# Constant products at the start of a hybrid encoder layer, and the small products of its triangular inverses in another order

## The chip, the cores and the metric

The kernel runs on one core of a Trainium2 chip. A core has a matrix engine (TensorE, PE in the profile), three engines for element work (VectorE or DVE, ScalarE or ACT, GpSimd or POOL) and queues for transfers (SP above all). Each engine works through its own list of instructions in order and waits on semaphores. TensorE reads operands from SBUF and writes to PSUM, which has eight banks of 128 partitions by 512 f32 values. The metric is the device time of one execution in microseconds. The kernel before takes 1374.57 us, the median of three runs (1373.78 to 1376.54).

## The reference

One layer on 512 positions of width 1024, in f32, conditioned by a vector c. Cut to what matters:

```python
c_act = silu(c);  mod = c_act @ w_ada + b_ada          # nine vectors of 1024
u = rmsnorm(h, norm_ffn1) * (1 + sc1) + sh1
h = h + 0.5 * g1 * swiglu(u, w_ffn1_up, w_ffn1_down)
u = rmsnorm(h, norm_mix) * (1 + sc2) + sh2
h = h + g2 * mixer(u)       # short gated convolution + bidirectional gated DeltaNet, merged by gates
u = rmsnorm(h, norm_ffn2) * (1 + sc3) + sh3
h = h + 0.5 * g3 * swiglu(u, w_ffn2_up, w_ffn2_down)
out = rmsnorm(h, norm_final)
# DeltaNet, per head and direction, in chunks:
a_mat = strict_lower(k_beta @ k.T * decay) + I
u, w = triangular_solve(a_mat, [v * beta, k_beta * exp(g)])
# then a scan over the chunks with the state S (128 x 128)
```

## The kernel before, in words

Channels lie on the 128 partitions, the 512 positions along the free axis. A large product is done in three 128x512 passes over operands that are split in a high and a low part (lines 186 to 188 in `product_steps`); weights come as 512 KB tiles (`weight`, line 169), ScalarE makes the high part (line 174) and VectorE the low part (line 176).

The start. SP loads h; ScalarE squares its eight tiles and VectorE adds them into `ssum` (line 134). TensorE spreads c over the partitions by two products with one row (line 138), and ScalarE applies silu to get `cs`. `rstd_bcast` sums the squares over the partitions by eight products with a single column (lines 220 and 223), VectorE divides (`ms`, line 225), GpSimd raises to the power -1/2 (`rs`, line 228) and TensorE spreads the result over all partitions (line 231) into the bank kq; ScalarE copies it to `bs` (line 893). Then a loop over the eight tiles k of the width begins (lines 896 to 919). For each k VectorE multiplies two tiles of w_ada with cs (line 150), adds the bias (154), makes the scale (157), t (line 908) and the low parts ul (912) and wfl (914); ScalarE makes wfh (903) and uh (911); TensorE does 24 passes (line 918) that accumulate eight outputs in all eight banks. The first feed-forward block follows without a break.

The mixer. The order of its tasks is written out by hand in `EMIT`: letters for building a head's operands (b), inverting (i), merging (p), scanning (s) and fillers (z, g, a, m, y); large projections run between the small products. Below that a scheduler in the language's framework sets each engine's order, so an edit of one task can move instructions of others. The eight PSUM banks are: three for acc, two for ch, and one each for tp, o and kq. `build` uses tp and kq for transposes (line 481) and o and kq for the products of keys and queries (lines 547 and 548), which VectorE reads (lines 552 and 556).

The inverses. For a head there are eight 128x128 triangular matrices (four chunks of 128 positions, two directions), treated as two 64-halves of two 32-blocks each. `invert` inverts the 32x32 diagonal blocks on VectorE (lines 582 and 584). `merge` joins them: VectorE transposes blocks (line 604); the first stage multiplies, for each half b and each matrix n, a 32x32 off-diagonal block by an inverse (line 610) into the bank tp and ScalarE copies the half out (line 612); the second stage multiplies from the other side, once for the inverse (line 618) and once for its transpose (line 620), again into tp with copies (622 and 624); then 64x64 products (lines 630, 636 and 637) join the halves. A half is the partitions 0 to 63 or 64 to 127. In TensorE's terms the first stage of half 0 reads rows 32 to 63 of the array and writes columns 0 to 31, that of half 1 reads rows 96 to 127 and writes columns 64 to 95. In the second stage line 618 reads rows 0 to 31 (half 1: 64 to 95) and writes columns 0 to 31 (64 to 95), line 620 reads the same rows and writes columns 32 to 63 (96 to 127). An f32 product is two passes in the profile, each with a weight load. After the merge `scan` runs the chain over the chunks (lines 668 to 702), and line 724 transposes the result.

Of the kernel before, what the change touches and what calls it, by code (L numbers as in the profile page):

```python
# [16 lines left out]
P = 128  # L17
T = 512
# [35 lines left out]
def tile_layer(  # L54
# [24 lines left out]
    pe, act, dve, pool = nc.tensor, nc.scalar, nc.vector, nc.gpsimd  # L79
# [13 lines left out]
    psx = open_pool(ctx, "psx", bufs=1, space=PSUM)  # L93
    psum_ch = open_pool(ctx, "psum_ch", bufs=CH, space=PSUM)

    def bank(tag="acc", pool_=None):
        return (pool_ or psum).tile([P, 512], F32, tag=tag, name=tag, **({"bufs": TP} if tag == "tp" else {}))


    ones = const.tile([P, P], F32, name="ones")  # L100
    pool.memset(ones[:], 1.0)
    ident = const.tile([P, P], F32, name="ident")
# [6 lines left out]
    start = ExitStack()  # L109
# [14 lines left out]
    ssum = [sm["p"].tile([P, T], F32, tag="ssum", bufs=1, name="ssum"), None]  # L124
# [11 lines left out]
    for i in range(2):  # L136
        ps = bank("o", psx) if i else bank("ch", psum_ch)
        pe.matmul(ps[:], ones[0:1, :], crow[:, i, :], start=True, stop=True)
        act.activation(out=cs[:, T * i : T * i + T], in_=ps[:], func=ACT.Silu)


    part = const.tile([P, 72], F32, name="part")
# [69 lines left out]
    def new_sums():  # L212
        return [sm["p"].tile([P, T], F32, tag="ssum", bufs=1, name="ssum"), None]

    def rstd_bcast(sums, t0, t1, tag):

        n = (t1 - t0) // P
        ps = bank("tp", psx)
        for i in range(n):
            pe.matmul(ps[:, i : i + 1], sums[0][:, t0 + i * P : t0 + (i + 1) * P], ones[:, 0:1], start=True,  # L220
                      stop=len(sums) == 1)
            if len(sums) == 2:
                pe.matmul(ps[:, i : i + 1], sums[1][:, i * P : (i + 1) * P], ones[:, 0:1], start=False, stop=True)  # L223
        ms = sm["p"].tile([P, NC], F32, tag="ms", name="ms")
        dve.tensor_scalar(out=ms[:, 0:n], in0=ps[:, 0:n], scalar1=1.0 / D, scalar2=EPS, op0=ALU.mult,  # L225
                          op1=ALU.add)
        rs = sm["p"].tile([P, NC], F32, tag="rs", name="rs")
        pool.tensor_tensor(out=rs[:, 0:n], in0=ms[:, 0:n], in1=mhalf[:, 0:n], op=ALU.pow)  # L228
        bc = bank(tag, psx)
        for i in range(n):  # L230
            pe.matmul(bc[:, i * P : i * P + P], rs[:, i : i + 1].to_broadcast([P, P]), ident[:], start=True, stop=True)  # L231
        return bc
# [86 lines left out]
    def mixer(st, u, h, post):  # L319
# [26 lines left out]
        with ExitStack() as dd:  # L346
# [17 lines left out]
            ps = bank("ch", psum_ch)  # L364
# [16 lines left out]
            ps = bank("tp", psx)  # L381
# [31 lines left out]
            ps = bank("tp", psx)  # L413
            for d in range(2):
                pe.matmul(ps[:, 32 * d : 32 * d + 32], tri[:, d, :], g[:, d].rearrange("p c h -> p (c h)"),
                          start=True, stop=True)
# [10 lines left out]
        with dn:  # L427
# [171 lines left out]
            def merge(s, tt):  # L599
                th, tht = tt  # L600
                nl = s["nl"][:].rearrange("p d c x -> p (d c) x")
                for b in range(4):
                    co = 32 * (b % 2)
                    dve.transpose(tht[32 * b : 32 * b + 32, :, co : co + 32], th[32 * b : 32 * b + 32, :, co : co + 32])
                ps = bank("tp", psx)
                w = one.tile([P, 8, 32], F32, tag="w", bufs=2, name="w")
                for b in range(2):
                    a0, d0 = 64 * b, 64 * b + 32
                    for n in range(8):
                        pe.matmul(ps[a0 : a0 + 32, 32 * n : 32 * n + 32], nl[d0 : d0 + 32, n, a0 : a0 + 32],  # L610
                                  tht[d0 : d0 + 32, n, 32:64], start=True, stop=True)
                    act.copy(w[a0 : a0 + 32].rearrange("p a b -> p (a b)"), ps[a0 : a0 + 32, 0:256])
                yield
                ps = bank("tp", psx)
                for b in range(2):
                    a0, d0 = 64 * b, 64 * b + 32
                    for n in range(8):
                        pe.matmul(ps[a0 : a0 + 32, 32 * n : 32 * n + 32], th[a0 : a0 + 32, n, 0:32],
                                  w[a0 : a0 + 32, n, :], start=True, stop=True)
                        pe.matmul(ps[d0 : d0 + 32, 32 * n : 32 * n + 32], w[a0 : a0 + 32, n, :],  # L620
                                  th[a0 : a0 + 32, n, 0:32], start=True, stop=True)
                    act.copy(tht[a0 : a0 + 32, :, 32:64],
                             ps[a0 : a0 + 32, 0:256].rearrange("p (a b) -> p a b", a=8))
                    act.copy(th[d0 : d0 + 32, :, 0:32],
                             ps[d0 : d0 + 32, 0:256].rearrange("p (a b) -> p a b", a=8))
                yield
                w2 = one.tile([64, 8, 64], F32, tag="w2", bufs=2, name="w2")
                ps = bank("tp", psx)
                for n in range(8):
                    pe.matmul(ps[0:64, 64 * n : 64 * n + 64], nl[64:128, n, 0:64], tht[64:128, n, :],  # L630
                              start=True, stop=True)
                act.copy(w2[:].rearrange("p a b -> p (a b)"), ps[0:64, :])
                yield
                ps = bank("tp", psx)
                for c in range(NC):
                    pe.matmul(ps[0:64, 64 * c : 64 * c + 64], th[0:64, c, :], w2[:, c, :], start=True, stop=True)
                    pe.matmul(ps[64:128, 64 * c : 64 * c + 64], w2[:, NC + c, :], th[0:64, NC + c, :],
                              start=True, stop=True)
# [12 lines left out]
                pool.tensor_tensor(out=f[0:64, NC:8, 0:64], in0=th[0:64, NC:8, :], in1=sc(rki, 0), op=ALU.mult)  # L651
                pool.tensor_tensor(out=f[64:128, NC:8, 64:128], in0=th[64:128, NC:8, :], in1=sc(rki, 64),
                                   op=ALU.mult)
                dve.tensor_tensor(out=f[64:128, NC:8, 0:64], in0=pv[64:128], in1=sc(rki, 64), op=ALU.mult)
                s["f"] = f
# [232 lines left out]

    lead["p"] = open_pool(first, "lead", bufs=6, side="right")
    u = new_u()  # L890
    bc = rstd_bcast(ssum, 0, T, "kq")
    bs = sp0.tile([P, T], F32, name="bs")
    act.copy(bs[:], bc[:])
    sp1 = open_pool(start, "start_raw", bufs=RAW0)
# [148 lines left out]
```

## Time and profile before

| what | value |
|---|---|
| median of three runs | 1374.57 us |
| profiled execution, its time | 1372.99 us |
| profiled execution, its span (first to last instruction) | 1371.2 us |
| TensorE busy | 1336.6 us, 97% |
| VectorE busy | 801.8 us, 58% |
| ScalarE busy | 566.3 us, 41% |
| L610, L618, L620: passes | 256 each, 191 ns each (median) |

The profile names an instruction by line, engine, operation and tiles (written <- read). A row of the timeline has its start, its duration, and in brackets the idle time of the engine before it with what ended it. Durations of passes overlap: the pitch of a stream is the distance of starts. "x16" joins rows that follow each other. A row of the windows view has the stretch, its length, the busy time of TensorE, weight loads, VectorE, ScalarE and GpSimd with the number of instructions, the granted clock of TensorE as a fraction, the share of the transfer engines and GB/s. A row of the waits view has who waited for whom, the sum, how often, and the longest.

### The profile page before, as it was taken

What the parts mean: (1) busy time and instruction counts of PE and PEld (TensorE: products, weight loads), DVE (VectorE), ACT (ScalarE), POOL (GpSimd) and SP (SyncE); (2) the same over time, 40 slices, a digit from 0 to 9 for tenths busy, and PEclk for the clock granted to TensorE, in tenths of its full rate; (3) what the DMA queues carried; (4) which work ended last, traced back from release to release, by engine and by line L of the source; (5) the groups of instructions that cost most, each with busy time, mean ns of one, the idle gap of its engine ahead of it and who ended that gap; (6) DMA issues with size and microseconds to landing.
All of it is one profiled execution on the core that took longest, in us unless ns stands there. A gap on an engine that the chain in (4) does not pass through costs nothing. (4 is left out here: it accounts for less than half of the span.)

```text
span 1371.2 us, 19599 instructions
## 1 busy us (share of the span) xinstructions
PE 1336.6 (97%) x7417; PEld 1109.4 (81%) x7417; DVE 801.8 (58%) x1745; ACT 566.3 (41%) x1150; POOL 65.3 (5%) x103
## 2 busy tenths in 40 slices
PE   6999999999999999999999999999999999999997
PEld 4888888888888888787787777788898888888886
DVE  6865555545467989756956774657653444443333
ACT  3333333222256773665464333545433333332230
POOL 0000000000010110121111001000000000000000
PEclk9999999999999999999999999999999999999998
DMA  8646556555433543433442242557412333332331
GB/s 316 225 155 196 171 198 192 174 177 167 151 128 101 161 129 116 128 102 104 147 112 96 80 130 86 179 195 251 166 47 92 127 133 110 124 118 85 100 109 64
DMA packets 80567, 193.46 MB, mean 141 GB/s; under 512 B 24857, under 2 KB 27097, under 8 KB 80346
## 3 DMA queue, kind: packets, MB, share of 16 engines
q1 hardware_dynamic: 64984, 164.29, 38.0%
q10 hardware_dynamic: 15490, 27.94, 5.9%
q8 instruction: 58, 0.95, 0.3%
q14 instruction: 35, 0.29, 0.1%
HBM read 171.19 MB, written 21.00 MB: 140 GB/s over the span
## 5 line engine op out<-in xcount | busy, mean ns | idle before, releaser
L186 PE MATMUL acc<-uh,hi 128*128 128x512 f32 (+1 forms) x1224 | 472.5, 386 | 2.6 <-DVE sps L397 0.9
L174 ACT CAST hi<-raw 128x512 fp32r<-128x512 f32 (+1 forms) x416 | 252.1, 612 | 533.8 <-PE acc L188 486.7
L187 PE MATMUL acc<-uh,lo 128*128 128x512 f32 (+1 forms) x1224 | 471.6, 386 | 0.3 <-DVE lo L176 0.3
L188 PE MATMUL acc<-ul,hi 128*128 128x512 f32 (+1 forms) x1224 | 471.6, 386 | 0.0
L176 DVE TENSOR_TENSOR lo<-raw,hi 128x512 fp32r<-128x512 f32 (+1 forms) x416 | 279.7, 679 | 293.9 <-ACT hi L174 292.1
L186 PEld LDWEIGHTS acc<-uh,hi 128*128 128x128 f32 x1224 | 230.5, 188 | 44.1 <-ACT cacc L439 1.1
L187 PEld LDWEIGHTS acc<-uh,lo 128*128 128x128 f32 x1224 | 230.5, 188 | 41.8 <-DVE lo L176 0.5
L188 PEld LDWEIGHTS acc<-ul,hi 128*128 128x128 f32 x1224 | 230.0, 188 | 41.7
L186 PE MATMUL acc<-gh,hi 128*128 128x512 f32 (+1 forms) x396 | 144.9, 366 | 0.0
L187 PE MATMUL acc<-gh,lo 128*128 128x512 f32 (+1 forms) x396 | 144.7, 365 | 0.0
L188 PE MATMUL acc<-gl,hi 128*128 128x512 f32 (+1 forms) x396 | 144.5, 365 | 0.0
L150 DVE SCALAR_TENSOR_TENSOR raw<-raw,cs 128x1024 f32<-128x1024 f32 x72 | 88.0, 1224 | 60.2 <-DMA raw<-w_ada 60.0
L187 PEld LDWEIGHTS acc<-gh,lo 128*128 128x128 f32 x396 | 74.4, 188 | 12.2
L186 PEld LDWEIGHTS acc<-gh,hi 128*128 128x128 f32 x396 | 74.4, 188 | 12.1
L188 PEld LDWEIGHTS acc<-gl,hi 128*128 128x128 f32 x396 | 74.4, 188 | 11.8
L444 DVE SCALAR_TENSOR_TENSOR cacc<-acc,cvd_sb,cacc 128x510 f32<-128x510 f32 (+1 forms) x96 | 70.7, 741 | 1.8 <-ACT cacc L439 1.2
L313 DVE TENSOR_TENSOR sa<-sa,acc 128x512 f32<-128x512 f32 x40 | 27.4, 686 | 35.1 <-PE acc L188 33.1
L228 POOL TENSOR_TENSOR rs<-ms,mhalf 128x2 f32<-128x2 f32 (+1 forms) x7 | 6.2, 891 | 836.2 <-DVE ms L225 836.2
L196 ACT CAST gh<-sa 128x512 fp32r<-128x512 f32 x44 | 27.4, 622 | 17.9 <-DVE sa L313 13.2
L206 ACT ACTIVATE sq<-h 128x512 f32<-128x512 f32 (+1 forms) x25 | 14.1, 563 | 47.6 <-DVE h L255 47.2
L197 DVE TENSOR_TENSOR gl<-sa,gh 128x512 fp32r<-128x512 f32 x44 | 30.4, 692 | 5.5 <-PE tp L918 2.1
L582 DVE TENSOR_TENSOR tmp<-A 96x30 f32<-96x30 f32 (+29 forms) x90 | 29.0, 322 | 1.2
(283 smaller groups left out, 1450.7 us busy)
## 6 DMA issues: line engine op xcount, KB each, us to landing
raw<-w_ada SPq DMA_DIRECT2D x72, 512.0 KB
raw<-w_in SPq DMA_DIRECT2D x60, 512.0 KB
raw<-w2u SPq DMA_DIRECT2D x44, 512.0 KB
raw<-w1u SPq DMA_DIRECT2D x36, 512.0 KB
raw<-w1d SPq DMA_DIRECT2D x16, 512.0 KB
raw<-w2d SPq DMA_DIRECT2D x16, 512.0 KB
wf<-w1f SPq DMA_DIRECT2D x8, 512.0 KB
dl<-nl SPq DMA_DIRECT2D x8, 512.0 KB
```

Of the source, the lines that this page charges most:

```text
L150: dve.scalar_tensor_tensor(out=raw[:], in0=raw[:], scalar=1.0, in1=cs[:], op0=ALU.mult, op1=ALU.mult, accum_out=part[:, n : n + 1])
L174: act.copy(hi[:], raw[:, k : k + n, :])
L176: dve.tensor_sub(lo[:], raw[:, k : k + n, :], hi[:].bitcast(F32))
L186: pe.matmul(ps[:, t0:t1], wh, rh[:, k0 + k, t0:t1], start=a, stop=False)
L187: pe.matmul(ps[:, t0:t1], wl, rh[:, k0 + k, t0:t1], start=False, stop=False)
L188: pe.matmul(ps[:, t0:t1], wh, rl[:, k0 + k, t0:t1], start=False, stop=b)
L196: act.copy(hi, src)
L197: dve.tensor_sub(lo, src, hi.bitcast(F32))
L206: act.activation(out=sq[:], in_=hk, func=ACT.Square)
L313: dve.tensor_mul(sa[:], sa[:], ps[1][:])
L444: dve.scalar_tensor_tensor(out=acc[:, lo:hi], in0=src[:, lo + o : hi + o], scalar=w[:, i : i + 1], in1=acc[:, lo:hi], op0=ALU.mult, op1=AL ...
L582: dve.tensor_tensor(out=tv, in0=A[:, j + 1 : 32, j : j + 1].to_broadcast([nb, n, j]), in1=A[:, j : j + 1, 0:j].to_broadcast([nb, n, j]), o ...
```

## The change

A helper issues products of two constants, the all-ones tile and the identity, into an acc bank that nobody reads before it is overwritten. Fourteen of them follow the products of line 138, nine stand between the sum of squares and its spreading (by the new argument `keep`, used at this one call), and eight follow the spreading. In `merge` the two halves of a stage write to a bank each, tp and kq, instead of both to tp; the products are issued matrix by matrix with the halves in turn, kept in that order, and the copies of both halves follow all products. The line numbers of what stands behind grow by 6 to 19.

```diff
+    def idle_work(n):
+
+        ps = bank()
+        for i in range(n):
+            pe.matmul(ps[:, 0:P], ident[:], ones[:], start=True, stop=True)
...
+    idle_work(14)
...
-    def rstd_bcast(sums, t0, t1, tag):
+    def rstd_bcast(sums, t0, t1, tag, keep=0):
...
+        if keep:
+            idle_work(keep)
...
-                ps = bank("tp", psx)
+
+                ps = [bank("tp", psx), bank("kq", psx)]
                 w = one.tile([P, 8, 32], F32, tag="w", bufs=2, name="w")
-                for b in range(2):
-                    a0, d0 = 64 * b, 64 * b + 32
-                    for n in range(8):
-                        pe.matmul(ps[a0 : a0 + 32, 32 * n : 32 * n + 32], nl[d0 : d0 + 32, n, a0 : a0 + 32],
-                                  tht[d0 : d0 + 32, n, 32:64], start=True, stop=True)
-                    act.copy(w[a0 : a0 + 32].rearrange("p a b -> p (a b)"), ps[a0 : a0 + 32, 0:256])
-                yield
+                rows = [(64 * b, 64 * b + 32, ps[b]) for b in range(2)]
+                for n in range(8):
+                    for a0, d0, pb in rows:
+                        i = pe.matmul(pb[a0 : a0 + 32, 32 * n : 32 * n + 32], nl[d0 : d0 + 32, n, a0 : a0 + 32],
+                                      tht[d0 : d0 + 32, n, 32:64], start=True, stop=True)
+                        if n or a0:
+                            tc.keep_in_program_order(i)
+                for a0, d0, pb in rows:
+                    act.copy(w[a0 : a0 + 32].rearrange("p a b -> p (a b)"), pb[a0 : a0 + 32, 0:256])
+                yield
+                ps = [bank("tp", psx), bank("kq", psx)]
...
+                for n in range(8):
+                    for a0, d0, pb in rows:
+                        i = pe.matmul(pb[a0 : a0 + 32, 32 * n : 32 * n + 32], th[a0 : a0 + 32, n, 0:32],
+                                      w[a0 : a0 + 32, n, :], start=True, stop=True)
+                        if n or a0:
+                            tc.keep_in_program_order(i)
+                        i = pe.matmul(pb[d0 : d0 + 32, 32 * n : 32 * n + 32], w[a0 : a0 + 32, n, :],
+                                      th[a0 : a0 + 32, n, 0:32], start=True, stop=True)
+                        tc.keep_in_program_order(i)
...
-    bc = rstd_bcast(ssum, 0, T, "kq")
+    bc = rstd_bcast(ssum, 0, T, "kq", 9)
+    idle_work(8)
```

At the start TensorE's list was this (L138 spreads c, L220 and L223 sum the squares, L231 spreads the result, L918 is the first large product):

```order
L138 MATMUL ch<-crow,ones 128x512
L138 MATMUL o<-crow,ones 128x512
L220 MATMUL tp<-ones,ssum 128x1
L223 MATMUL tp<-ones,sq_124 128x1
L220 MATMUL tp<-ones,ssum 128x1
L223 MATMUL tp<-ones,sq_124 128x1
L220 MATMUL tp<-ones,ssum 128x1
L223 MATMUL tp<-ones,sq_124 128x1
L220 MATMUL tp<-ones,ssum 128x1
L223 MATMUL tp<-ones,sq_124 128x1
L231 MATMUL kq<-ident,rs 128x128 x4
L918 MATMUL acc<-uh,wfh 128x512 x3
```

And now, from the end of the same sum of squares (L228 and L231 are the former L220 and L223, L241 the former L231, L937 the former L918; L103 is the helper):

```order
L228 MATMUL tp<-ones,ssum 128x1
L231 MATMUL tp<-ones,sq_124 128x1
L103 MATMUL acc<-ones,ident 128x128 x9
L241 MATMUL kq<-ident,rs 128x128 x4
L103 MATMUL acc<-ones,ident 128x128 x8
L937 MATMUL acc<-uh,wfh 128x512 x3
```

The 31 new products are 62 passes in TensorE's list; the lists of VectorE, ScalarE and SP are the same as before up to the mixer's inverses.

In the mixer, TensorE's list around the change of halves in the second stage of the first merge was this (t_10 is the tile of the inverses, w the result of the first stage):

```order
L618 MATMUL tp<-w,t_10_3337 32x32
L620 MATMUL tp<-t_10_3337,w 32x32
L188 MATMUL acc<-ul,hi 128x512
L186 MATMUL acc<-uh,hi 128x512
L187 MATMUL acc<-uh,lo 128x512
L188 MATMUL acc<-ul,hi 128x512
L618 MATMUL tp<-w,t_10_3337 32x32
L620 MATMUL tp<-t_10_3337,w 32x32
```

Now (L632 and L636 are the former L618 and L620, L194 the former L186):

```order
L632 MATMUL tp<-w,t_10_3371 32x32
L636 MATMUL tp<-t_10_3371,w 32x32
L632 MATMUL kq<-w,t_10_3371 32x32
L636 MATMUL kq<-t_10_3371,w 32x32
L632 MATMUL tp<-w,t_10_3371 32x32
L636 MATMUL tp<-t_10_3371,w 32x32
L632 MATMUL kq<-w,t_10_3371 32x32
L636 MATMUL kq<-t_10_3371,w 32x32
L194 MATMUL acc<-uh,hi 128x512
```

The two halves' blocks of 16 products each, with large passes between them, became one block of 32 in which the halves take turns. Over the eight heads the 32 blocks of 32x32 products became 27 pieces. In five of the eight first stages the first product stands alone ahead of large passes and 15 follow later; in five of the eight second stages the first two products do so, and one of these has another product between its later parts.

More of the change, by code (lines that the diff above doesn't have):

```diff
@@ L613, in merge @@
-                yield
[L614 to L621, printed above, removed]
+                rows = [(64 * b, 64 * b + 32, ps[b]) for b in range(2)]
@@ new lines, in merge @@
+                yield
+                ps = [bank("tp", psx), bank("kq", psx)]
+                rows = [(64 * b, 64 * b + 32, ps[b]) for b in range(2)]
+                for n in range(8):
[7 more added lines that the diff above has]
+                        tc.keep_in_program_order(i)
@@ L622, in merge @@
+                for a0, d0, pb in rows:
                     act.copy(tht[a0 : a0 + 32, :, 32:64],
-                             ps[a0 : a0 + 32, 0:256].rearrange("p (a b) -> p a b", a=8))
+                             pb[a0 : a0 + 32, 0:256].rearrange("p (a b) -> p a b", a=8))
                     act.copy(th[d0 : d0 + 32, :, 0:32],
-                             ps[d0 : d0 + 32, 0:256].rearrange("p (a b) -> p a b", a=8))
+                             pb[d0 : d0 + 32, 0:256].rearrange("p (a b) -> p a b", a=8))
```

## The prediction

> **What bounds the kernel now.** I read the page's busy line first, then three stretches of the windows view, then the list of what TensorE waited for.
>
> ```profile
> span 1371.2 us, 19599 instructions
> PE 1336.6 (97%) x7417; PEld 1109.4 (81%) x7417; DVE 801.8 (58%) x1745; ACT 566.3 (41%) x1150; POOL 65.3 (5%) x103
> ```
> ```profile
> 0.00:21.00 21.00, 9.64 (x29) 6.68 (x30) 9.87 (x16) 9.48 (x16) 2.60 (x8) 1.00 0.92 338
> 21.00:360.00 339.00, 339.00 (x1481) 279.04 (x1482) 203.43 (x335) 110.01 (x179) 0.00 (x0) 1.00 0.58 187
> 540.00:880.00 340.00, 331.26 (x2563) 266.27 (x2562) 227.94 (x674) 168.49 (x440) 44.78 (x68) 0.99 0.37 112
> ```
> ```profile
> PE tp L220 <- DVE ssum L134: 4.5, 1, 4.5
> PE tp L724 <- DVE on L719: 3.4, 4, 1.6
> PE ch L685 <- DVE yw L682: 1.8, 1, 1.8
> ```
>
> TensorE is the bound: from 21 to 360 us it is busy all 339 us, and in the stretch of the inverses (540 to 880) it lacks only 8.74 of 340 us. Time taken out of its queue there should come out of the whole. Three of its largest holes lie in the first 21 us, 4.5 us long here and 2.26 and 2.22 in the rows below: the places where the change puts constant products. The other two rows are the scan's chain in the mixer. What follows at 21 us is a full queue, so a start that comes earlier stays earlier.
>
> **The start, before.** These are the timeline rows on the way to the first large product (start, duration, engine, line).
>
> ```profile
> 4.25 1.91 PE L138 MATMUL o<-crow,ones 1*128 1x512 f32 x2
> 10.63 0.59 PE L220 MATMUL tp<-ones,ssum 128*128 128x1 f32 x2 [4.47 <-DVE ssum L134]
> 14.56 1.85 POOL L228 TENSOR_TENSOR rs<-ms,mhalf 128x4 f32<-128x4 f32 x1 [13.17 <-DVE ms L225]
> 16.46 2.08 PE L231 MATMUL kq<-ident,rs 128*128 128x128 f32 x8 [2.26 <-POOL rs L228]
> 20.76 1.65 PE L918 MATMUL acc<-uh,wfh 128*128 128x512 f32 x3 [2.22 <-ACT uh L911]
> 23.91 0.63 PE L918 MATMUL tp<-uh,wfh 128*128 128x512 f32 x1
> 24.34 1.06 PE L918 MATMUL acc<-ul,wfh 128*128 128x512 f32 x3
> 25.70 0.40 PE L918 MATMUL o<-ul,wfh 128*128 128x512 f32 x1
> 25.93 0.40 PE L918 MATMUL kq<-ul,wfh 128*128 128x512 f32 x1
> ```
> A 128x512 pass takes 0.43 us (23.91 to 24.34) and later 0.23 (25.70 to 25.93): TensorE runs at half speed until about 24.8, four microseconds after dense work began at 20.76. (The clock column shows 1.00 for 0 to 21, so here the pitch must be read.) Later in the program the same thing can be seen after a hole:
>
> ```profile
> 635.79 0.79 PE L685 MATMUL ch<-yw,kt 128*128 128x128 f32 x2 [1.76 <-DVE yw L682]
> 637.24 0.63 PE L188 MATMUL acc<-ul,hi 128*128 128x512 f32 x1
> 637.66 0.63 PE L186 MATMUL acc<-uh,hi 128*128 128x512 f32 x1
> 639.51 0.39 PE L186 MATMUL acc<-uh,hi 128*128 128x512 f32 x1
> 639.74 0.40 PE L187 MATMUL acc<-uh,lo 128*128 128x512 f32 x1
> ```
> After 1.76 us without work the pitch is 0.42, and 0.23 again within 3.8 us. So holes do cost speed, and dense work brings it back in under 4 us.
>
> **What the constant products do.** One of them is a 128x128 f32 product, two passes. L231 gives its slow price: 8 passes in 2.08, with the last one's drain, so near 0.22 each. Its fast price comes from 14 such passes between these two starts, 1.63 / 14 = 0.116:
>
> ```profile
> 605.63 1.79 PE L697 MATMUL o<-y,at 128*128 128x128 f32 x14
> 607.26 0.83 PE L702 MATMUL ch<-S,qT 128*128 128x128 f32 x6
> ```
> The 14 products (28 passes) begin when L138 ends, at 6.16. All slow they last 28 x 0.22 = 6.2 us, to 12.3, and hold up the sum of squares (ready at 10.63) by 1.7. If speed comes four microseconds after 2.41, when L138 began, they end near 9.5; if L138's one-row products do not count and the four run from 6.16, near 11.3. So 0 to 0.7 us late.
> The ladder L220/L223 is 16 passes, 10.63 to 14.24, 0.22 each; at 0.116 it saves 1.7. The 9 products (18 passes) then fill POOL's power with DVE's step ahead of it (the 2.26 hole): 2.1 us fast, hidden; 4.0 slow, 1.7 late. L231's 8 passes save 8 x 0.104 = 0.8 to 1.0. The 8 products (16 passes) sit ahead of L918 in TensorE's queue: 1.9 fast, inside the 2.22 hole of copy, t and uh; 3.5 slow, 1.3 late. L918's first writes to the accumulators now also wait for those products to leave the same banks; the work is on the same engine just ahead, so I count it in their 1.9.
> Fast throughout, bs is ready 2.7 us sooner. The first 24 passes of L918 would gain another two by speed, but VectorE supplies the next step:
>
> ```profile
> 26.38 0.75 DVE L908 SCALAR_TENSOR_TENSOR t<-h,ga,bs 128x512 f32<-128x512 f32 x1
> 26.64 1.05 ACT L903 CAST wfh<-wf 128x1024 fp32r<-128x1024 f32 x1 [5.00 <-PE tp L918]
> 27.60 1.35 ACT L911 ACTIVATE uh<-t,mod 128x512 fp32r<-128x512 f32 x2
> 28.37 0.50 PE L918 MATMUL acc<-uh,wfh 128*128 128x512 f32 x1
> ```
> VectorE runs without a hole from bs to this t, so t moves with bs, 2.7. ScalarE's cast stands ahead of uh and waits for TensorE; with TensorE fast it no longer delays uh (0.47). The second step then starts 2.7 to 3.1 sooner, and TensorE waits about 1.9 us before it instead of 0.3. That is where the speed of the first step goes. From there the queue is full.
> Bounds of the start: -3.1 (always fast), +4.7 (1.7 + 1.7 + 1.3, always slow). Between them: the ladder's one-column passes, 1.9 us, may count as a hole like the one at 635.79, the 9 run slow, and only about -1 is left. I take -2.3, nearest to the fast end, since dense work of 6 us outlasts the 4 that both rows show.
>
> **What the interleaving does.** The 32x32 products stand in 32 blocks, 16 of L610 and 16 of L618/L620, each alone between large passes. One block of each kind:
>
> ```profile
> L610 PE MATMUL tp<-t,nl x256: 184/191/212, 558.3 to 828.3; 32*32 32x32 f32 x128
> 585.13 0.39 PE L187 MATMUL acc<-uh,lo 128*128 128x512 f32 x1
> 585.45 0.69 PE L610 MATMUL tp<-t,nl 32*32 32x32 f32 x16
> 586.06 0.50 PE L188 MATMUL acc<-ul,hi 128*128 128x512 f32 x1
> 586.40 0.40 PE L186 MATMUL acc<-uh,hi 128*128 128x512 f32 x1
> ```
> ```profile
> 569.26 0.19 PE L618 MATMUL tp<-w,t 32*32 32x32 f32 x1
> 569.26 0.19 PE L620 MATMUL tp<-t,w 32*32 32x32 f32 x1
> 569.29 0.19 PE L618 MATMUL tp<-w,t 32*32 32x32 f32 x1
> 569.30 0.19 PE L620 MATMUL tp<-t,w 32*32 32x32 f32 x1
> 569.83 0.50 PE L186 MATMUL acc<-uh,hi 128*128 128x512 f32 x1
> ```
> L610: 16 passes, 0.61 us from first to next. L618/L620: 32 passes in the same time, because a pass of each starts within 10 ns and the next two 0.033 later: two products side by side, on the same rows and different columns of the array. Around a block the neighbours lose 0.2 (585.13 to 585.45 is 0.32 and 586.06 to 586.40 0.34, where 0.23 is normal). All blocks: 32 x (0.62 + 0.20) = 26.2 us of TensorE.
> After the change the order has 27 pieces (some first products are cut off by large ones). If the two halves, which use different rows, run side by side too, a stage is 16 slots of 0.033 for either kind: 16 stages x 0.53 = 8.4, and 27 x (0.09 tail + 0.20) = 7.8; 16.2, a saving of 10.0. No row shows different rows at once, so bounds: if four passes per slot are too many and two is the most, the second kind takes twice that, 4.2 more, saving 5.8; if halves never overlap, 8.4 more, saving 1.6. I take 7.8, between the first two, since the pairs show that the sequencer can start passes closer than one per slot.
> [...]
> The price of the second bank: kq is also used for the transposes of v and for half of the key products; these hold it until VectorE has read it.
>
> ```profile
> L552 DVE SCALAR_TENSOR_TENSOR nl<-kq,st,ef x16: 332/340/347, 447.6 to 744.4; 128x128 f32<-128x128 f32 x16
> L556 DVE TENSOR_TENSOR at<-kq,ef x8: 405/412/416, 448.6 to 745.0; 128x256 f32<-128x256 f32 x8
> ```
> That is 4 x 0.34 + 2 x 0.41 = 2.2 us per use. The new order puts large passes between such a use and the merge, which covers most of it. The copies of a first half also no longer run under the second half's products; 0.36 each on ScalarE (41% busy), covered by the large passes that follow. And the rest of this stretch is reordered a little on all queues. For these together I give back 1.8, a quarter of the saving, bounded by 0 and by rival three. Interleaving: -6.0.
>
> **Sum.** -2.3 - 6.0 = -8.3. The profiled execution took 1372.99 (span 1371.2 and 1.8 around it): 1364.7. The median of the runs is 1.6 above it: **1366.3**. Its own range, with -1.0 to -3.1 and -3.5 to -10: 1361.5 to 1370.
>
> **Rivals.** One: the halves do not run side by side, because the array takes one group of rows at a time (0.13) or because starts cannot come closer than they do now (0.04). For it: no row shows it; against it: pairs on other columns. Either way a second half's passes need slots of their own: start -2.3, blocks -1.6 less a quarter, -1.2: 1371.1. [...] Two: the saved time returns as waits elsewhere in the mixer, since the scan's chain through VectorE already opens holes (L724 3.4, L685 1.8), and only the start is left, itself held back by the ladder: about 1373.5. Against it: the 97.4% busy stretch. Three, slower: kq. Each of 16 stages claims it; a claim that comes right after a key product stops the whole queue, large passes included, for up to 2.2 us, and over 1.76 the half clock follows. It decides from 8.3 / 16 = 0.5 us per claim; at 0.8 us, where 12.8 is lost, the result is 1379.1. Against it: most claims in the order stand several large passes behind the last use.
>
> **How the numbers follow.** Forecast 0.60, rival one 0.17, two 0.12, three 0.11. What can be told from no change is 0.2%, 2.75 us. Faster: 0.60 but for 0.02, and most of one, 0.14: 0.72. Same: 0.02, 0.03 and most of two, 0.11: 0.16. Slower: 0.11 and 0.01. The range 1361.5 to 1374.5 takes in the forecast, one and most of two.
>
> **What would show it.** L918's first pass near 18.0 at a pitch of 0.23 from the first; the ladder's passes 0.11 apart; a wait of about 2 us before the second step. If the constant passes are 0.22 apart up to 12 us, the start is lost. In the mixer: passes of the two halves within 10 ns, a whole second-kind stage in 0.62 to 0.9. If it takes 1.2, rival one. If waits on kq of TensorE appear among the first ten, rival three.

## The result and the profile after

The change makes the kernel faster: 1362.86 us, the median of 4 runs (1362.34 to 1364.63), against 1375.55 for the kernel before on the same chip (4 runs, 1373.78 to 1377.19). The ratio is 0.9913, with a 95% interval of 0.9898 to 0.9928: 9.9 to 14.0 us less. The forecast was 8.3 us less, 1366.3.

First the page of the changed kernel, its two lines on the span and the engines, then the same three stretches of the windows view as before (stretch, its length, busy time of PE, PEld, DVE, ACT and POOL with instruction counts, PEclk, DMA share, GB/s).

```profile
span 1361.8 us, 19714 instructions
PE 1333.8 (98%) x7479; PEld 1110.7 (82%) x7479; DVE 800.7 (59%) x1745; ACT 564.3 (41%) x1150; POOL 64.3 (5%) x103
```
```profile
0.00:21.00 21.00, 17.98 (x96) 14.85 (x97) 11.09 (x19) 10.12 (x16) 2.60 (x8) 1.00 0.93 347
21.00:360.00 339.00, 337.68 (x1483) 278.03 (x1482) 200.84 (x332) 108.66 (x179) 0.00 (x0) 1.00 0.59 188
540.00:880.00 340.00, 330.30 (x2623) 266.86 (x2622) 234.48 (x689) 173.31 (x453) 43.88 (x68) 0.99 0.39 118
```

TensorE is busy for 18.0 of the first 21 us where it was for 9.6, and lacks 1.3 us between 21 and 360. Those 1.3 are one wait, in the timeline rows of the changed kernel's start:

```profile
6.13 6.09 PE L103 MATMUL acc<-ones,ident 128*128 128x128 f32 x28
12.06 0.28 PE L228 MATMUL tp<-ones,ssum 128*128 128x1 f32 x2
13.77 2.25 PE L103 MATMUL acc<-ones,ident 128*128 128x128 f32 x18
16.16 1.16 PE L241 MATMUL kq<-ident,rs 128*128 128x128 f32 x8
17.16 1.95 PE L103 MATMUL acc<-ones,ident 128*128 128x128 f32 x16
19.54 0.96 PE L937 MATMUL acc<-uh,wfh 128*128 128x512 f32 x3 [0.43 <-ACT uh L930]
26.72 0.98 PE L937 MATMUL acc<-uh,wfh 128*128 128x512 f32 x3 [1.32 <-ACT uh L930]
```

All 28 first passes ran slow here (6.09 / 28 = 0.217 each), so the ladder began at 12.06 instead of 10.63. It ended at 13.77, and everything after it ran fast: 18 passes in 2.25 and L241's 8 in 1.16 (2.08 before). The first large product begins at 19.54 (20.76 before), at full speed; the second step at 26.72 (28.37 before).

A second-kind stage of the interleaved products, from the timeline of the changed kernel:

```profile
565.77 0.21 PE L632 MATMUL tp<-w,t 32*32 32x32 f32 x1
...
565.98 0.19 PE L632 MATMUL tp<-w,t 32*32 32x32 f32 x1
565.98 0.19 PE L636 MATMUL tp<-t,w 32*32 32x32 f32 x1
566.00 0.19 PE L632 MATMUL kq<-w,t 32*32 32x32 f32 x1
566.00 0.19 PE L636 MATMUL kq<-t,w 32*32 32x32 f32 x1
566.01 0.19 PE L632 MATMUL tp<-w,t 32*32 32x32 f32 x1
...
566.52 0.50 PE L194 MATMUL acc<-uh,hi 128*128 128x512 f32 x1
```

Both kinds and both halves start within 0.03 us of each other, four passes per slot (565.98 to 566.01). The whole stage of 64 passes takes 0.75 us (565.77 to 566.52); before it was two blocks of 0.62, each with its own pair of neighbours. Added up over the timeline in the same way (from the first 32x32 start to the next other start), the 32 blocks of before hold 19.7 us, the 27 pieces now 12.4.

The list of TensorE's waits has no kq of a merge in it. Its row for yw, the second:

```profile
PE ch L703 <- DVE yw L700: 2.8, 2, 1.9
```

How far the profiled executions are apart at marks of the program (start of the first or last such instruction, us):

| mark | before | after | difference |
|---|---|---|---|
| second k-step | 28.37 | 26.72 | -1.65 |
| first 32x32 product | 558.3 | 557.0 | -1.3 |
| scan's first output product (L702, L720) | 605.0 | 602.4 | -2.6 |
| last 64x64 product | 869.2 | 857.4 | -11.8 |
| last y transposed (L724, L742) | 903.5 | 891.5 | -12.0 |
| last output rows (L967, L986) | 1367.5 | 1358.1 | -9.4 |

So the gain is made in the stretch of the inverses, and 2.6 of it is gone again at the end, in this execution (at 1364.63 the longest of its four). That end, from the last y to the end of the span, holds the same work in every kernel here and took 465.9 to 473.5 us in their fourteen profiles, so 2.6 there says nothing of the change.

### The profile page after: what moved, and what is told of

Its sections match the earlier page's. It is cut to its first block, busy times and chain, and to the rows that moved or that the text cites. A ratio compares the mean times of both kernels' runs of the same rounds, so it can differ in the third digit from the quotient of the medians.

```text
span 1361.8 us, 19714 instructions
## 1 busy us (share of the span) xinstructions
PE 1333.8 (98%) x7479; PEld 1110.7 (82%) x7479; DVE 800.7 (59%) x1745; ACT 564.3 (41%) x1150; POOL 64.3 (5%) x103
## 4 chain that ended last, share of the span: by engine, by line
PE 73%; issue 9%; DMA 7%; DVE 5%; ACT 3%; POOL 1%; ACTq 0%; POOLq 0%; SPq 0%; DVEq 0%
PE acc L196 20%; PE acc L194 20%; PE acc L195 20%; DMA msb<-gtd 2%; DVE lo L184 1%; PE acc L937 1%; PE ch L692 1%; DVE cacc L454 1%; DMA raw<-w2u 1%; PE ch L703 1%; PE ch L937 1%; PE o L715 1%; ACT hi L182 1%; PE ch L720 1%; DMA msa<-gtd 1%
## 5 line engine op out<-in xcount | busy, mean ns | idle before, releaser
L194 PE MATMUL acc<-uh,hi 128*128 128x512 f32 (+1 forms) x1224 | 472.3, 386 | 2.1 <-DVE sps L407 0.9
L194 PEld LDWEIGHTS acc<-uh,hi 128*128 128x128 f32 x1224 | 230.4, 188 | 43.8 <-ACT cacc L449 1.1
L194 PE MATMUL acc<-gh,hi 128*128 128x512 f32 (+1 forms) x396 | 144.9, 366 | 0.0
L194 PEld LDWEIGHTS acc<-gh,hi 128*128 128x128 f32 x396 | 74.4, 188 | 12.1
L214 ACT ACTIVATE sq<-h 128x512 f32<-128x512 f32 (+1 forms) x25 | 14.1, 563 | 47.6 <-DVE h L265 47.3
L594 DVE TENSOR_TENSOR A<-A,tmp 96x30 f32<-96x30 f32 (+29 forms) x90 | 29.0, 322 | 1.5
```

Source lines behind the costliest of these rows:

```text
L194: pe.matmul(ps[:, t0:t1], wh, rh[:, k0 + k, t0:t1], start=a, stop=False)
L594: dve.tensor_tensor(out=A[:, j + 1 : 32, 0:j], in0=A[:, j + 1 : 32, 0:j], in1=tv, op=ALU.add)
```

## The experiments

My theory after the result: the interleaving gives about 10 us, because two halves run side by side, and the start gives the rest. The rivals: the start gives most; the halves overlap only because each has its own bank; the gain comes from fewer switches between large and small products. All ratios are to the kernel before on the same chip; a ratio of 0.001 is 1.4 us.

| run | what it is | median, us | ratio, 95% interval |
|---|---|---|---|
| start_only | constant products, merge of before | 1373.35 | 0.9995, 0.9978 to 1.0012 |
| mix_only | interleaving, no constant products | 1363.78 | 0.9925, 0.9907 to 0.9943 |
| one_bank | change, both halves in tp | 1368.05 | 0.9959, 0.9944 to 0.9973 |
| half_after_half | change, no interleaving | 1365.65 | 0.9944, 0.9927 to 0.9961 |
| before_z2 | before, two z buffers | 1373.66 | 1.0005, 0.9991 to 1.0019 |
| start_z2 | start_only, two z buffers | 1375.07 | 1.0014, 1.0000 to 1.0027 |
| after_z2 | change, two z buffers | 1361.78 | 0.9925, 0.9908 to 0.9942 |
| one_bank_z2 | one_bank, two z buffers | 1365.65 | 0.9950, 0.9938 to 0.9962 |
| before_zpool | before, z loaded by GpSimd | 1371.60 | 0.9991, 0.9975 to 1.0008 |
| start_zpool | start_only, z loaded by GpSimd | 1371.08 | 0.9976, 0.9960 to 0.9991 |
| after_zpool | change, z loaded by GpSimd | 1359.11 | 0.9898, 0.9879 to 0.9917 |
| one_bank_zpool | one_bank, z loaded by GpSimd | 1361.72 | 0.9916, 0.9897 to 0.9936 |

### Each part alone

start_only takes the change's first part and leaves `merge` as it was; mix_only the other way round.

```diff
 # start_only: after, with the old body of merge()
-                ps = [bank("tp", psx), bank("kq", psx)]
+                ps = bank("tp", psx)
 ...
 # mix_only: before, with the new body of merge(); no idle_work()
```

> The constant products of the change, with the merge of before. In the changed kernel's profile the second k-step starts at 26.72 us instead of 28.37, and the first product of the inverses at 557.0 instead of 558.3. Theory (the interleaving gives about 10 us of the 12.7, the start the rest): 1.3 to 3.0 us below the kernel before, ratio 0.9978 to 0.9991. Rival (most of the extra gain over the forecast came from the start, because TensorE keeps its full speed there in most executions): 5 us or more below, ratio 0.9964 or less. If the ladder L228/L231 starts at about 10.6 instead of 12.06, the constant products ran fast in this execution.

> The interleaved products with two banks, without any constant product. Theory: about 10 us below the kernel before (8.5 to 11.5), ratio 0.9917 to 0.9938, and with the other half it adds up to the whole change. Rival (the two parts help each other, or the start gives most): 6 us below or less, ratio 0.9956 or more.

The interleaving alone gives 10.3 us (7.8 to 12.8), as the theory had it. That is the whole edit of `merge`; what of it comes from the halves running side by side, the next section asks. The constant products alone give 0.7, between a gain of 3.0 and a loss of 1.6: the rival is out, and the theory's 1.3 to 3.0 is not shown either. Yet in the profile the start is there: the second step begins at 25.70, 2.67 sooner than before, and the scan's first output product 2.3 sooner (602.7). The last 64x64 product stands only 0.4 sooner (868.8). Apart from the constant products, the two programs have the same passes in the same order on TensorE, so the starts of one pass can be compared: start_only is 2.5 us ahead at 360, 2.25 at 620, 0.1 at 640 and 0.4 behind at 660. ScalarE's wait in before, in the stretch from 600 to 700 (TensorE's 1.8 behind it, L685, is in the prediction):

```profile
ACT y L679 <- DMA ybd<-z: 2.9, 1, 2.9
```

And start_only's timeline there:

```profile
625.95 0.44 ACTq L742 DMA_DIRECT2D ybd<-z  x1
634.21 0.37 ACT L689 ACTIVATE y<-ch,st 128x128 f32<-128x128 f32 x1 [4.44 <-DMA ybd<-z]
635.02 0.80 PE L695 MATMUL ch<-yw,kt 128*128 128x128 f32 x2 [3.26 <-DVE yw L692]
636.47 0.63 PE L196 MATMUL acc<-ul,hi 128*128 128x512 f32 x1
...
639.03 0.63 PE L194 MATMUL acc<-uh,hi 128*128 128x512 f32 x1
```

ScalarE's queue holds the load of a head's z, which waits for the last head's ybd to land; y stands behind it, VectorE's yw behind y, TensorE behind yw (the hold, from here on). In start_only the transfer of ybd was issued 2.25 us sooner (625.95 against 628.20) and landed only 0.8 sooner. So TensorE came to the same place earlier and waited longer, 3.26 instead of 1.76, and the half clock that follows (in before the granted clock is 0.51 from 637.20 to 639.20) lasted longer as well (a 128x512 pass still takes 0.63 at 639.03; in before it takes 0.39 from 639.51). The two rows of the windows view over the whole stretch, from the first 32x32 product to the start of the last transpose of y (L724), before and start_only:

```profile
558.30:903.50 345.20, 336.13 (x2608) 270.63 (x2609) 226.88 (x675) 174.77 (x460) 45.79 (x69) 1.00 0.38 116
```
```profile
556.00:903.70 347.70, 337.08 (x2607) 272.00 (x2607) 227.03 (x675) 174.73 (x460) 45.78 (x69) 0.99 0.37 115
```

start_only needs 2.5 us more for the same work: 0.95 as busy time (the slow passes) and 1.55 as idle time. That is what it had gained. Why the same transfer took longer (6.4 us in before, 7.9 here, from its issue to the load behind it) these rows do not show.

### One bank, and no interleaving

```diff
 # one_bank
-                ps = [bank("tp", psx), bank("kq", psx)]
+                ps = [bank("tp", psx)] * 2
 # half_after_half, both stages
-                for n in range(8):
-                    for a0, d0, pb in rows:
+                for a0, d0, pb in rows:
+                    for n in range(8):
```

> The changed kernel with both 64-halves' products written to one bank (tp) in the same interleaved order. Without the second bank the order has 19 contiguous pieces of 32x32 products instead of 27. Theory A (the halves run side by side only because each has a bank of its own): the passes of the two halves start 0.03 us apart, a second-kind stage lasts about 1.1 us instead of 0.6, and 8 stages x 0.53 + 8 x 0.5 = 8 us are lost less the 8 pieces x 0.29 = 2.3: about 6 us above the changed kernel, ratio to before near 0.995. Rival B (different rows are enough): starts within 10 ns as with two banks, and the 8 pieces fewer save up to 2.3 us: 0 to 2.3 us below the changed kernel, ratio 0.989 to 0.991.

> The changed kernel with its two banks, but all products of one half ahead of those of the other; the order has 26 contiguous pieces of 32x32 products (27 in the changed kernel, 32 before). Theory (the gain is the running side by side of two halves): 16 stages x 0.53 = 8.4 us of it are lost, so 7 to 9 us above the changed kernel, ratio to before near 0.997. Rival (the gain comes from fewer switches between large and small products and from the place of the copies): within 2 us of the changed kernel, ratio near 0.991.

A stage of one_bank from its timeline, and one of half_after_half:

```profile
583.40 0.21 PE L632 MATMUL tp<-w,t 32*32 32x32 f32 x1
583.40 0.21 PE L636 MATMUL tp<-t,w 32*32 32x32 f32 x1
583.41 0.21 PE L632 MATMUL tp<-w,t 32*32 32x32 f32 x1
583.42 0.21 PE L636 MATMUL tp<-t,w 32*32 32x32 f32 x1
...
584.08 0.49 PE L195 MATMUL acc<-uh,lo 128*128 128x512 f32 x1
```
```profile
564.12 0.21 PE L632 MATMUL tp<-w,t 32*32 32x32 f32 x1
...
564.53 0.21 PE L632 MATMUL kq<-w,t 32*32 32x32 f32 x1
...
564.62 0.19 PE L632 MATMUL tp<-w,t 32*32 32x32 f32 x1
...
565.16 0.50 PE L195 MATMUL acc<-uh,lo 128*128 128x512 f32 x1
```

With one bank the halves run side by side just as well: 64 passes in 0.68 us. Without interleaving the same 64 take 1.04. All pieces together: 12.4 us in 27 pieces with the change, 10.9 in 19 with one bank, 18.2 in 26 without interleaving. So the own bank is not what makes them overlap, and the order is; fewer switches do not shorten the pieces, since half_after_half has 26 of them and 5.9 us more.

The times do not follow the pieces alone. half_after_half is 7.7 us below the kernel before (5.4 to 10.0), 4.3 above the change by the two ratios (1.1 to 7.4); I had expected 7 to 9 above, from 16 stages x 0.53. By the times alone the rival (within 2) is not ruled out; the 5.9 us of the pieces are what speaks against it. The 0.53 of a second half was too much: half after half also saves a tail per stage (1.04 against 2 x 0.62). Read the other way, a kernel whose halves hardly overlap already has 7.7 of the change's 12.0 us, and its pieces are only 1.5 us shorter than before's. What else it gains is shown in part: its first ybd goes out at 618.50 and the load of z at 620.52, so the hold of ScalarE and TensorE's hole near 635 are not there. (It has a hole of its own later: TensorE waits 2.1 for yah at L804.) And one_bank is 5.6 below (3.7 to 7.7), 6.3 above the change, where its pieces are the shortest of all and the rival had forecast 0 to 2.3 below the change. Its own waits show one reason:

```profile
633.61 0.58 ACT L650 COPY w<-tp 64x512 f32<-64x512 f32 x1 [5.45 <-DMA ybd<-z]
...
634.89 0.79 PE L703 MATMUL ch<-yw,kt 128*128 128x128 f32 x2 [3.27 <-DVE yw L700]
```

It is the same load of z again, with other work behind it; passes are slow after this hole too (0.43 apart at 636.3).

### The load of z: two buffers

The z tile has one buffer, so the load could be waiting for that. Two buffers need 2 KB per partition, and r and yw gave up one each.

```diff
-SL, NL, RAW, ZB, CP, FLB = 5, 5, 3, 1, 6, 2
+SL, NL, RAW, ZB, CP, FLB = 5, 5, 3, 2, 6, 2
-                            rt = wk.tile([P, P], F32, tag="r", bufs=4, name="r")
+                            rt = wk.tile([P, P], F32, tag="r", bufs=3, name="r")
-                            yw = wk.tile([P, P], F32, tag="yw", bufs=4, name="yw")
+                            yw = wk.tile([P, P], F32, tag="yw", bufs=3, name="yw")
```

> The kernel before with two buffers for z (ZB 2) and, to make room for it, three instead of four buffers each for r and yw. With one buffer, ScalarE's load of a head's z waits until the last head's ybd has been written, and everything queued on ScalarE stands behind it: y at L679 waited 2.9 us for ybd, and TensorE 1.76 behind that, at 635.79, with the half clock after it until 639.2 (worth another 1.7). Theory: that wait and the dip are gone, 1.7 to 3.5 us below the kernel before, ratio 0.9975 to 0.9988. Rival (the wait moves to the next thing that is late, VectorE): no change.

> The constant products alone (merge of before) with two buffers for z and three for r and yw. In the run of the constant products alone the second k-step came 2.67 us sooner and the first output product of the scan (L712) 2.3 us sooner, but the last 64x64 product only 0.4: the wait for ybd had grown from 2.9 to 4.4 us, and TensorE's hole from 1.76 to 3.26. Theory (the start's gain is lost to that wait): 1.5 to 3 us below the same kernel without constant products, which runs beside it; ratio to before about 0.996. Rival (the gain is lost elsewhere or is not there in most executions): within 1 us of it.

> The changed kernel with two buffers for z and three for r and yw. In its profile TensorE waits 1.9 us behind yw at the same place, and ScalarE 2.7 for ybd. Theory: 1.5 to 3.5 us below the changed kernel, ratio to before 0.988 to 0.990. Rival (the hole comes from VectorE's own queue): as the changed kernel, 0.9913.

> Both halves in one bank, with two buffers for z. In the run with one bank the halves ran side by side (64 passes in 0.68 us, blocks 10.95 us in all against 12.36 with two banks), yet the program was longer, with a wait of 5.45 us for ybd on ScalarE and a hole of 3.27 on TensorE. Theory (the bank is not what it lost): that loss is gone, and 19 pieces instead of 27 now count: 0 to 3 us below the changed kernel with two z buffers. Rival (the one bank itself costs 4 to 6 us through waits on tp): 4 us or more above it.

The forecasts fell. Nothing became faster that can be told, and the wait is where it was, in before_z2 and in start_z2:

```profile
ACT y L679 <- DMA ybd<-z: 3.0, 1, 3.0
```
```profile
ACT y L689 <- DMA ybd<-z: 4.4, 1, 4.4
```

after_z2 is 1.6 us above the change by the two ratios and one_bank_z2 1.2 below one_bank, each with 3 us of uncertainty; one_bank_z2 is 3.4 above after_z2 (0.6 to 6.3), between the forecasts of 0 to 3 below it and 4 or more above it.

That does not clear the buffer, though. ScalarE's queue in before_z2 shows what the second one did:

```profile
469.34 0.81 ACTq L728 DMA_DIRECT2D z<-zd  x2
628.98 0.44 ACTq L732 DMA_DIRECT2D ybd<-z  x1
635.38 0.33 ACTq L728 DMA_DIRECT2D z<-zd  x1
```

Two loads go out at 469, where the kernel before has one (468.50). The load behind the first ybd is now the third, where it was the second. Each load was moved one head forward in the queue and again needs the buffer that the ybd just issued still reads. With one buffer the second load stands behind the first ybd, with two the third: that is what a wait for the buffer gives. So the buffer remains the likely reason, and these runs did not take the wait away; the load would have to be issued later, or from another queue.

The runs do repeat the reading of start_only: with constant products 4.4 and, on TensorE, 3.2, without 3.0 and 1.8. The second step came 3.3 us sooner (25.91 against 29.23), the last 64x64 product 0.5 (869.6 against 870.1).

### The load of z: another queue

```diff
-                nc.scalar.dma_start(z[:], zd[:, hd, :])
+                nc.gpsimd.dma_start(z[:], zd[:, hd, :])
```

> The kernel before with the load of z issued by GpSimd's queue instead of ScalarE's; one buffer for z as before. With two buffers the wait stayed (3.0 us for ybd on ScalarE, a hole of 1.8 on TensorE), so it is not the buffer; it is what stands behind the waiting load on ScalarE's queue. Theory: with the load on another queue, y and yw are no longer held, the hole of 1.76 at 635.8 and the half clock behind it are gone: 1.7 to 3.5 us below the kernel before, ratio 0.9975 to 0.9988. Rival (GpSimd's queue, or z itself, is then as late for something else): no change.

> The constant products alone (merge of before), with the load of z on GpSimd's queue. In both runs of the constant products alone the hole behind ybd was 3.2 us where it was 1.8 without them. Theory (the start's gain is lost to that wait): now it reaches the end, 1.5 to 2.7 us below the same kernel without constant products, and the stretch from the first 32x32 product to the scan's last output is as long in both. Rival (another stretch takes it): within 1 us of it.

> The changed kernel with the load of z on GpSimd's queue. Theory: 1 to 3.5 us below the changed kernel, ratio to before 0.988 to 0.991. Rival: as the changed kernel (0.9913), or above it, because the order of TensorE's work differs in places.

Now GpSimd's queue holds the load, and GpSimd has little else to do (5% busy before). In before_zpool the first ybd goes out at 627.97, and the load behind it late again:

```profile
635.01 0.63 POOL L728 DMA_DIRECT2D z<-zd  x1 [2.85 <-DVE r L670]
```

ScalarE's wait for ybd before y is gone, and so are TensorE's hole near 635 and the half clock after it (what is left behind yw in this stretch is 0.7 us, at 665); the stretch from the first 32x32 product to the last y takes 341.9 us instead of 345.2. The windows of before_zpool and then start_zpool:

```profile
558.10:900.00 341.90, 334.47 (x2609) 268.91 (x2609) 227.42 (x675) 173.95 (x459) 50.68 (x76) 1.00 0.38 116
```
```profile
556.30:899.30 343.00, 334.48 (x2607) 268.93 (x2608) 228.14 (x675) 173.88 (x459) 50.14 (x76) 1.00 0.38 116
```

The two now have the same busy time to 0.01 us: the constant products change nothing in the work of that stretch. start_zpool still waits 1.1 us longer in it: for VectorE's transposes of the inverses 1.4 against 0.5, for yw 1.2 against 0.7, and 0.8 for a copy on ScalarE that the other does not wait for. So the hold was not the only place where an early start is lost: of the 3.3 us that the second step gained, 1.8 are left at the first 32x32 product and 0.7 at the last y. As times, before_zpool is 1.2 us below the kernel before (3.4 below to 1.1 above), so its forecast of 1.7 to 3.5 is not shown, and start_zpool is 2.1 below before_zpool (3.1 either way): its forecast of 1.5 to 2.7 holds the middle and is not shown either.

after_zpool is 14.0 us below the kernel before (11.4 to 16.6), 2.1 more than the change by the two ratios, with intervals that overlap. Its ratio is the lowest here, but the forecast of 1 to 3.5 below the change is not shown.

> Both halves in one bank, and the load of z on GpSimd's queue. With one bank the 32x32 products took 10.9 us in 19 pieces, against 12.36 in 27 pieces with two banks, and yet that program was 4 to 6 us longer, with ScalarE held 5.4 us by the load of z that waits for ybd, and TensorE 3.3 behind it and slow for some 3 us more. Theory (that hold is what one bank lost, by the order it happens to give, not the bank): 4 to 6 us below the run with one bank, at 0 to 3 us below the changed kernel with the load of z on GpSimd's queue, ratio to before 0.988 to 0.990. Rival (the one bank itself costs it, through claims of tp that wait for copies): still 3 us or more above that kernel, ratio 0.992 or more, with waits on tp among TensorE's first ten that two banks do not show.

one_bank_zpool is 11.5 us below (8.8 to 14.1), 5.9 better than one_bank by the two ratios (2.6 to 9.2): the hold is most of what one bank had lost. It does not get below after_zpool (2.5 above, 3.7 either way), though it has 8 pieces fewer. In TensorE's list, two waits of products that write tp are longer than after_zpool's (0.4 for the first, the second not listed):

```profile
PE tp L621 <- DVE t L614: 1.4, 4, 0.8
PE tp L648 <- ACT t L642: 1.2, 4, 0.4
```

Both rows wait for operands, what VectorE transposes and what ScalarE copies out of tp, so whether the single bank causes them is not shown. Half speed after a hole of 1.44 near 571 (0.43 from pass to pass) is also in this profile and not in after_zpool's. Which of the two is better can't be told at this size.

## Why the prediction was right, and where not

**Right: direction, and the mechanism of the interleaving.** The step "if the two halves, which use different rows, run side by side too" was the open one, and they do. Of the full price, 26.2 - 16.2 = 10.0, 8.4 came: 7.4 measured in the pieces (19.7 to 12.4) and 1.0 estimated for 5 switches fewer at the 0.20 that I had read. The pieces hold 12.4 and not 8.4 + 27 x 0.09 = 10.8, because a second-kind stage of 60 to 64 passes in one piece takes 0.65 to 0.86 and not 0.62, and each of the ten pieces of first products that are cut off takes 0.15 to 0.18. I took 7.8, so that step was near.

**Wrong in size: "I give back 1.8".** This was the price of kq, of the copies and of the new order. The waits of TensorE in the stretch from the first 32x32 product to the last y add up to 8.2 us in mix_only and 8.8 before, so nothing was given back in waits. The change is 12.0 below where 8.3 was forecast; -8.4 instead of -6.0 is the larger part of that miss, and mix_only's 10.3 (7.8 to 12.8) agrees with 8.4. The passes of both halves start close together in the change's profile: four within 0.02 us (565.98 to 566.00), and 49 starts from 565.98 to 566.40, four every 0.03 on average.

**The start: right at 28 us, wrong at the end.** The forecast was 2.3 sooner, between 1.0 and 3.1. In the four pairs that differ only by the constant products, the second step came 1.53 (the change against mix_only), 2.67, 3.32 and 3.31 us sooner. Its terms went otherwise than worked out, though. "0 to 0.7 us late" for the ladder was 1.43 in the profile of the change, where all 28 passes ran slow; in nine other kernels with the same start these 28 passes took 4.75 to 6.11 us. The 9 and the 8 products did hide in their holes in nine of these ten profiles (in one_bank the 9 ran slow), and the wait before the second step is there, 1.3 us where 1.9 was worked out.

The step that failed is the sentence "What follows at 21 us is a full queue, so a start that comes earlier stays earlier." In start_only it holds to 360 us and to the first scan (602.7 against 605.0), and then not: the stretch of the inverses had 8.7 us of idle time, and some of that ends with a transfer, not with TensorE's own work. At the last y, of 2.67, 3.32 and 3.31 us nothing, nothing and 0.7 are left, and 0.7 of 1.53 in the change against mix_only. The same four pairs, as times: 0.7 less, 1.2 more, 2.1 less, 1.6 less, each with 2 to 3 us of uncertainty; their mean, 0.8 less, is uncertain by 1.4. So what reaches the end is most likely less than the 2.3 that was forecast, and can't be told from nothing.

**The rivals.** One (no overlap) is out: 0.75 a stage, not 1.2. Three (kq) is out: no kq of a merge among the waits. Two was stated for the wrong half: "the saved time returns as waits elsewhere in the mixer" is what became of the start, while the interleaving kept its gain. It named the right chain, L685, behind which the ybd wait was found; its row stood among the three waits quoted first.

**The sum.** 8.4 for the interleaving and 0.8 for the start make 9.2, below the interval of the change (9.9 to 14.0) and inside that of the interleaving alone. What the rest is, the runs leave open. One candidate can be seen in the profiles but not timed: before, the half clock after the hole at 635.79 cost some 1.7 us (3.4 us at half speed), and it is missing in the change, as the last section shows, and in mix_only, whose hole there is also shorter:

```profile
634.36 0.49 PE L693 MATMUL ch<-yw,kt 128*128 128x128 f32 x2 [0.60 <-DVE yw L690]
```

In mix_only's profile the stretch of the inverses takes 333.2 us where it took 345.2: 8.4 for the pieces and switches, 1.2 for the shorter hole and 1.7 for the half clock make 11.3 of these 12.0. In the change's own profile the hole is as long as before (1.92) and only the half clock is missing. The forecast has no term for this: as far as it counts, part of the gain's size is luck, and half_after_half's 7.7 us point the same way. (The 3.5 at the small end of the forecast's range, too, stands there without a working.)

## What to carry to other kernels

Small products on different rows of the array are worth putting side by side in the order of instructions, alternating between the row groups: here 64 passes took 0.75 us that way (0.68 in one bank) and 1.04 half after half. A bank of their own is not needed for that, though the kernel with one bank was not the faster one here. A queue that is 97% full over hundreds of microseconds still lets an early start go to waste if one of its waits ends with a transfer (in start_only 2.67 us, of which nothing was left at the last y): before counting a shift as kept, follow each wait in that stretch to what lands last. A load that must wait belongs on a queue with nothing urgent behind it: that paid 5.9 us where the hold was 5.45, and could not be told from nothing in the other kernels.

## What was not expected of the hardware

**The clock after a hole depends on more than its length.** Before, 1.76 us without work were followed by passes 0.42 apart (granted clock 0.51 from 637.20 to 639.20). In the profile of the change the hole at the same place was 1.92, and the passes after it run at full speed (634.51 to 634.74: 0.23; granted clock 1.00 from 634.50 to 638.00):

```profile
633.73 0.49 PE L703 MATMUL ch<-yw,kt 128*128 128x128 f32 x2 [1.92 <-DVE yw L700]
...
634.51 0.39 PE L194 MATMUL acc<-uh,hi 128*128 128x512 f32 x1
634.74 0.40 PE L195 MATMUL acc<-uh,lo 128*128 128x512 f32 x1
```

Holes of 3.26 and 3.27 (start_only, one_bank) were followed by half speed. Near 571 the hole is 1.44 in one_bank and in one_bank_z2, with full speed after it in the first and half speed in the second (passes 0.23 and 0.43 apart):

```profile
571.79 0.49 PE L557 MATMUL o<-kT 128*128 128x128 f32 x2 [1.44 <-DVE at L566]
...
573.02 0.40 PE L196 MATMUL acc<-ul,hi 128*128 128x512 f32 x1
```
```profile
571.55 0.73 PE L557 MATMUL o<-kT 128*128 128x128 f32 x2 [1.44 <-DVE at L566]
...
573.79 0.63 PE L196 MATMUL acc<-ul,hi 128*128 128x512 f32 x1
```

So the prediction's "over 1.76 the half clock follows" is no rule either way, and what decides which speed follows a hole, no run here shows.

**Passes behind products of one row were slow, and in one run passes behind products of one column were slow again.** In the change L144's one-row products kept TensorE busy from 2.45 to 6.1, and the 28 passes behind them were still slow, to the last one (6.09 us in all; 6.11 in one_bank_z2). In the other eight kernels with constant products the 28 took 4.75 to 5.78, where 0.116 each would make 3.2. In one of the ten, one_bank, speed had come by the end of the 28 (5.28 in all): the ladder's one-column passes, from 11.70 on, stand 0.11 apart. The passes that follow the ladder, 1.8 us after its start, are slow again:

```profile
5.98 5.28 PE L103 MATMUL acc<-ones,ident 128*128 128x128 f32 x28
11.46 0.38 PE L228 MATMUL tp<-ones,ssum 128*128 128x1 f32 x2 [0.20 <-DVE ssum L140]
13.27 3.88 PE L103 MATMUL acc<-ones,ident 128*128 128x128 f32 x18
```

The 18 passes took 3.88, 0.216 each. That was a bound of the prediction ("the ladder's one-column passes, 1.9 us, may count as a hole"), and slow passes behind the ladder stand in one of ten profiles.

**Passes of the other row group overtake.** In half_after_half all products of tp stand ahead of those of kq in the program, yet passes into kq start at 564.53, before the last ones into tp (up to 564.62). So the starts of two row groups need not keep the program's order.
